# RMS norm on one core: storing the first half tile between the second and the third load, with half tiles alternating from there

## Chip, cores and metric

The kernel runs on one core of one Trainium2 chip. The metric is the device time of one execution in microseconds.

## The reference

The input `x` is 16 x 1024 x 512 in float32, so 16,384 rows of 512 elements and 33.55 MB. Every row is divided by its root mean square and multiplied by `gamma`.

```python
def reference(x, gamma):
    eps = 1e-5
    rms = np.sqrt(np.mean(x ** 2, axis=-1, keepdims=True) + eps)
    return (x / rms * gamma).astype(np.float32)
```

Each byte is read once and written once, 67.1 MB in all, with little arithmetic on it.

## The kernel before

The rows are cut into four tiles of 128 partitions x 32 rows, 8.39 MB each. Three buffers ("slots") hold tiles 0, 1 and 2, and tile 3 goes into slot 0 again. Every load and store is issued by SyncE, in program order. A half tile (16 rows per partition, 4.19 MB) is the unit in which I count below; "store 1a" is the store of the first half of tile 1.

```python
    load(0, 0, 0, 16)          # load(tile, slot, first row, last row)
    load(0, 0, 16, 32)
    load(1, 1, 0, 32)
    load(2, 2, 0, 32)
    ...
    def compute(slot, r0, r1):
        for g in range(r0, r1, G):                 # groups of 8 rows
            ...
            if (g // G) % 2:                       # odd group: two wide squares into PSUM (2 buffers)
                for h in range(0, G, H):
                    sq = psum.tile([P, H, D], fp32, name="sq")
                    nc.scalar.activation(out=sq, in_=slots[slot][:, g + h : g + h + H, :], func=AF.Square)
                    nc.vector.tensor_reduce(out=ss[:, h : h + H], in_=sq, ...)
            else:                                  # even group: eight row squares with their sums, ScalarE alone
                for r in range(G):
                    nc.scalar.activation(out=sq_scratch, ..., func=AF.Square, accum_out=ss[:, r : r + 1])
            nc.scalar.activation(out=rms, in_=ss, func=AF.Sqrt, ...)        # the root, ScalarE
            nc.vector.reciprocal(out=rstd, in_=rms)
            for r in range(G):
                nc.vector.scalar_tensor_tensor(...)                         # one row scaled, in place

    compute(0, 0, 32)
    store(0, 0, 0, 32)
    compute(1, 0, 16)
    store(1, 1, 0, 16)
    load(3, 0, 0, 16)
    load(3, 0, 16, 32)
    compute(1, 16, 32)
    store(1, 1, 16, 32)
    compute(2, 0, 32)
    store(2, 2, 0, 32)
    ...                                            # tile 3 in two halves
```

`sq`, the result of a wide square, has two buffers in PSUM, an on-chip memory: a third wide square waits until VectorE has summed the first.

A scheduler decides in which order each engine gets its instructions. It keeps the data dependences and is otherwise free, so the order on ScalarE and VectorE is not the order of the source.

Of the kernel before, what the change touches and what calls it, by code (L numbers as in the profile page):

```python
# [1 line left out]

# [4 lines left out]


@with_exitstack
def kernel(  # L10
    ctx: ExitStack,
    tc: tile.TileContext,
    x: bass.AP,
    gamma: bass.AP,
    out: bass.AP,
):
    nc = tc.nc
    P = nc.NUM_PARTITIONS
    eps = 1e-5
    fp32 = mybir.dt.float32  # L20
    AF = mybir.ActivationFunctionType
    OP = mybir.AluOpType

    xf = x.flatten_outer_dims()
    of = out.flatten_outer_dims()
    N, D = xf.shape
    R = 32
    G = 8
    H = 4
    assert N == 4 * P * R  # L30

    xv = xf.rearrange("(t p r) d -> t p r d", p=P, r=R)
    ov = of.rearrange("(t p r) d -> t p r d", p=P, r=R)

    const = ctx.enter_context(tc.tile_pool(name="const", bufs=1))
    stats = ctx.enter_context(tc.tile_pool(name="stats", bufs=4))
    psum = ctx.enter_context(tc.tile_pool(name="psum", bufs=2, space=bass.MemoryType.PSUM))

    slots = [const.tile([P, R, D], fp32, name=f"slot{i}") for i in range(3)]

    def load(t, slot, r0, r1):
        nc.sync.dma_start(out=slots[slot][:, r0:r1], in_=xv[t][:, r0:r1])

    def store(t, slot, r0, r1):
        nc.sync.dma_start(out=ov[t][:, r0:r1], in_=slots[slot][:, r0:r1])

    load(0, 0, 0, 16)
    load(0, 0, 16, 32)
    load(1, 1, 0, 32)
    load(2, 2, 0, 32)  # L50

    gamma_row = const.tile([1, D], fp32)
    nc.scalar.dma_start(out=gamma_row, in_=gamma.unsqueeze(0))
    ones_col = const.tile([1, P], fp32)
    nc.vector.memset(ones_col, 1.0)  # L55
    gamma_psum = psum.tile([P, H, D], fp32, name="sq")
    nc.tensor.matmul(gamma_psum[:, 0], ones_col, gamma_row, start=True, stop=True)  # L57
    gamma_b = const.tile([P, D], fp32)
    nc.vector.tensor_copy(out=gamma_b, in_=gamma_psum[:, 0])  # L59

    eps_t = const.tile([P, 1], fp32)
    nc.vector.memset(eps_t, eps)  # L62
    sq_scratch = const.tile([P, D], fp32)

    def compute(slot, r0, r1):
        for g in range(r0, r1, G):
            ss = stats.tile([P, G], fp32, name="ss")
            rms = stats.tile([P, G], fp32, name="rms")
            rstd = stats.tile([P, G], fp32, name="rstd")
            if (g // G) % 2:  # L70
# [3 lines that stand above are left out]
                    nc.vector.tensor_reduce(  # L74
                        out=ss[:, h : h + H], in_=sq, axis=mybir.AxisListType.X, op=OP.add
                    )
            else:
                for r in range(G):
                    nc.scalar.activation(  # L79
                        out=sq_scratch,  # L80
                        in_=slots[slot][:, g + r, :],
                        func=AF.Square,
                        accum_out=ss[:, r : r + 1],
                    )
            nc.scalar.activation(out=rms, in_=ss, func=AF.Sqrt, bias=eps_t, scale=1.0 / D)  # L85
            nc.vector.reciprocal(out=rstd, in_=rms)  # L86
            for r in range(G):
                nc.vector.scalar_tensor_tensor(  # L88
                    out=slots[slot][:, g + r, :],
                    in0=slots[slot][:, g + r, :],  # L90
                    scalar=rstd[:, r : r + 1],
                    in1=gamma_b,
                    op0=OP.mult,
                    op1=OP.mult,
                )

    compute(0, 0, 32)
    store(0, 0, 0, 32)
    compute(1, 0, 16)
    store(1, 1, 0, 16)  # L100
    load(3, 0, 0, 16)
    load(3, 0, 16, 32)
    compute(1, 16, 32)
    store(1, 1, 16, 32)
    compute(2, 0, 32)
    store(2, 2, 0, 32)
    compute(0, 0, 16)
    store(3, 0, 0, 16)
    compute(0, 16, 32)
    store(3, 0, 16, 32)  # L110


# [1 line left out]
_INS = ['x', 'gamma']  # L114
_OUTS = [((16, 1024, 512), 'float32')]


# [23 lines left out]
```

## Time and profile before

| What | Value |
|---|---|
| time | 162.38 us median of 3 (162.14 to 162.44) |
| VectorE busy | 123.4 us, 77% of the span |
| the SyncE queue's share of the 16 DMA engines | 97.9% |
| first half tile landed | 12.80 us |
| last store issued, landed | 147.90 us, about 159.5 us |

These are the head of the page of the kernel before and its DMA queue table (packets, megabytes, share of the span of the 16 engines):

```profile
span 160.6 us, 402 instructions
PE 2.0 (1%) x2; PEld 0.5 (0%) x2; DVE 123.4 (77%) x163; ACT 79.9 (50%) x162; POOL 0.2 (0%) x4
...
q1 hardware_dynamic: 1728, 67.11, 97.9%
q14 instruction: 2, 0.02, 0.0%
```

The next are waits of the kernel before: first VectorE's, then those of SyncE as it issues transfers (who waited for what: total us, times, longest).

```profile
DVE ss L74 <- ACT sq L73: 10.4, 1, 10.4
DVE rstd L86 <- ACT rms L85: 9.8, 4, 5.4
```

```profile
SPq L45 <- DVE slot L88: 113.7, 6, 28.3
...
SPq L136 <- DMA out_dram<-slot: 11.3, 2, 9.6
```

Two things end nearly together. The queue is busy from start to end. And the last store, which waits for VectorE's last multiply, is issued at 147.90 us; with 0.33 us to issue it and 11.3 us of waiting at the end, it lands at 159.5 us. VectorE is idle mainly for two reasons (and after its last multiply): it waits 10.4 us for the first data, and in all 9.8 us for ScalarE's root (line 86), one of these waits being 5.4 us.

This is VectorE's timeline in the kernel before where it goes from tile 1 to tile 2 (start, duration, operation; an idle time would stand in brackets at the end of the line):

```profile
82.67 0.26 DVE L86 RECIPROCAL rstd<-rms 128x8 f32<-128x8 f32 x2
82.89 10.69 DVE L88 SCALAR_TENSOR_TENSOR slot<-slot,rstd,gamma_b 128x512 f32<-128x512 f32 x16
93.50 4.48 DVE L74 TENSOR_REDUCE ss<-sq 128x4 f32<-128x2048 f32 x2
97.89 0.26 DVE L86 RECIPROCAL rstd<-rms 128x8 f32<-128x8 f32 x2
```

There is no bracket: VectorE does not wait here.

```profile
117.04 0.34 SPq L45 DMA_DIRECT2D out_dram<-slot  x1
...
147.90 0.33 SPq L45 DMA_DIRECT2D out_dram<-slot  x1
```

### The profile page before, as it was taken

The numbers are of one execution on the slowest core, as the hardware profiler recorded it, in microseconds if no ns is written. First come the engines' busy times: TensorE is split into PE (matmuls) and PEld (weight loads), VectorE is DVE, ScalarE is ACT, GpSimd is POOL, SyncE is SP. The second block draws the span as 40 slices with busy tenths as digits, with TensorE's granted clock in tenths as the row PEclk, the third lists the DMA queues.
The fourth block names the chain that finished last, engine by engine and source line by source line (L and its number), as shares of the span: only waits on it lengthen the run. The fifth ranks groups of instructions, "written<-read, shape, count | busy, mean of one in ns | idle before, by whom it ended". The sixth has DMA issues, their size and how long they took to land.

```text
span 160.6 us, 402 instructions
## 1 busy us (share of the span) xinstructions
PE 2.0 (1%) x2; PEld 0.5 (0%) x2; DVE 123.4 (77%) x163; ACT 79.9 (50%) x162; POOL 0.2 (0%) x4
## 2 busy tenths in 40 slices
PE   4000000000000000000000000000000000000000
PEld 1000000000000000000000000000000000000000
DVE  0101909999999509999999999998999999998000
ACT  3008999930580999995099314003998960000000
POOL 0000000000000000000000000000000000000000
DMA  7999999969969997997999999999997997999993
GB/s 262 392 408 498 400 408 506 522 261 522 522 263 522 506 278 345 441 522 310 473 392 416 465 416 416 473 416 408 457 547 310 506 490 310 416 465 408 433 457 155
DMA packets 1732, 67.13 MB, mean 418 GB/s; under 512 B 193, under 2 KB 193, under 8 KB 194
## 3 DMA queue, kind: packets, MB, share of 16 engines
q1 hardware_dynamic: 1728, 67.11, 97.9%
q14 instruction: 2, 0.02, 0.0%
q10 hardware_dynamic: 2, 0.00, 0.0%
HBM read 33.56 MB, written 33.55 MB: 418 GB/s over the span
## 4 chain that ended last, share of the span: by engine, by line
DVE 71%; ACT 12%; DMA 8%; issue 1%; DVEq 0%
DVE slot L88 52%; DVE ss L74 18%; DMA slot<-in_x_dram 8%; ACT sq_scratch L79 6%; ACT sq L73 4%; DVE rstd L86 1%; ACT L85 1%; ACT rms L85 1%; DVEq L136 0%
## 5 line engine op out<-in xcount | busy, mean ns | idle before, releaser
L88 DVE SCALAR_TENSOR_TENSOR slot<-slot,rstd,gamma_b 128x512 f32<-128x512 f32 x128 | 85.7, 746 | 0.1
L79 ACT ACTIVATE sq_scratch<-slot 128x512 f32<-128x512 f32 x64 | 40.0, 625 | 13.9 <-DMA slot<-in_x_dram 12.6
L74 DVE TENSOR_REDUCE ss<-sq 128x4 f32<-128x2048 f32 x16 | 36.1, 2276 | 10.5 <-ACT sq L73 10.4
L73 ACT ACTIVATE sq<-slot 128x2048 f32<-128x2048 f32 x16 | 29.8, 1860 | 4.9 <-DVE ss L74 4.9
L85 ACT ACTIVATE rms<-ss,eps_t 128x8 f32<-128x8 f32 x16 | 4.4, 297 | 37.4 <-DVE ss L74 37.2
L79 ACT ACTIVATION_READ_ACCUMULATOR sq_scratch<-slot 128x1 f32 x64 | 11.9, 187 | 0.0
L86 DVE RECIPROCAL rstd<-rms 128x8 f32<-128x8 f32 x16 | 2.8, 188 | 9.8 <-ACT rms L85 9.8
L59 DVE COPY gamma_b<-sq 128x512 f32<-128x512 f32 x1 | 0.7, 692 | 3.2 <-PE sq L57 3.2
L57 PE MATMUL sq<-gamma_row,ones_col 1*128 1x512 f32 x2 | 2.0, 1122 | 2.2 <-DMA gamma_row<-in_gamma_dram 2.2
L79 ACT ACT_TABLE_LOAD x1 | 1.3, 1283 | 1.3 <-PEq L125 1.3
L85 ACT ACT_TABLE_LOAD x1 | 1.3, 1283 | 0.0
L55 DVE MEMSET ones_col<- 1x128 f32 x1 | 0.2, 165 | 0.8 <-PEq L125 0.8
L57 PEld LDWEIGHTS sq<-gamma_row,ones_col 1*128 1x128 f32 x2 | 0.5, 305 | 2.1 <-issue 2.1
L125 POOL MEMSET const-bfloat16-1.0<- 128x1 bf16 x1 | 0.1, 102 | 0.0
L125 POOL MEMSET const-uint8-127<- 128x1 uint8 x1 | 0.1, 102 | 0.0
L125 POOL MEMSET const-float32-0.0<- 128x1 f32 x1 | 0.1, 99 | 0.2 <-issue 0.2
L125 POOL MEMSET const-float32-1.0<- 128x1 f32 x1 | 0.1, 99 | 0.0
L62 DVE MEMSET eps_t<- 128x1 f32 x1 | 0.1, 59 | 0.0
## 6 DMA issues: line engine op xcount, KB each, us to landing
slot<-in_x_dram SPq DMA_DIRECT2D x4, 4096.0 KB, 19.3
out_dram<-slot SPq DMA_DIRECT2D x4, 4096.0 KB, 18.0
slot<-in_x_dram SPq DMA_DIRECT2D x2, 50.5
out_dram<-slot SPq DMA_DIRECT2D x2, 27.6
gamma_row<-in_gamma_dram ACTq DMA_DIRECT2D x1, 2.0 KB
```

The source lines that it names most:

```text
L55: nc.vector.memset(ones_col, 1.0)
L57: nc.tensor.matmul(gamma_psum[:, 0], ones_col, gamma_row, start=True, stop=True)
L59: nc.vector.tensor_copy(out=gamma_b, in_=gamma_psum[:, 0])
L62: nc.vector.memset(eps_t, eps)
L73: nc.scalar.activation(out=sq, in_=slots[slot][:, g + h : g + h + H, :], func=AF.Square)
L74: nc.vector.tensor_reduce(out=ss[:, h : h + H], in_=sq, axis=mybir.AxisListType.X, op=OP.add)
L79: nc.scalar.activation(out=sq_scratch, in_=slots[slot][:, g + r, :], func=AF.Square, accum_out=ss[:, r : r + 1],)
L85: nc.scalar.activation(out=rms, in_=ss, func=AF.Sqrt, bias=eps_t, scale=1.0 / D)
L86: nc.vector.reciprocal(out=rstd, in_=rms)
L88: nc.vector.scalar_tensor_tensor(out=slots[slot][:, g + r, :], in0=slots[slot][:, g + r, :], scalar=rstd[:, r : r + 1], in1=gamma_b, op0=O ...
L125: nc = _bacc.Bacc("TRN2", target_bir_lowering=False, num_devices=1)
```

## The change

The intent is to begin storing early: the first half of tile 0 is stored before tile 2 is loaded, and from there loads and stores of half tiles alternate in the queue.

```diff
     load(0, 0, 0, 16)
     load(0, 0, 16, 32)
     load(1, 1, 0, 32)
-    load(2, 2, 0, 32)
 ...
-    compute(0, 0, 32)
-    store(0, 0, 0, 32)
+    compute(0, 0, 16)
+    store(0, 0, 0, 16)
+    load(2, 2, 0, 32)
+    compute(0, 16, 32)
+    store(0, 0, 16, 32)
+    load(3, 0, 0, 16)
     compute(1, 0, 16)
     store(1, 1, 0, 16)
-    load(3, 0, 0, 16)
     load(3, 0, 16, 32)
     compute(1, 16, 32)
     store(1, 1, 16, 32)
```

No arithmetic changes. The queue's order goes from `L0a L0b L1 L2 | S0 S1a L3a L3b S1b S2 S3a S3b` to `L0a L0b L1 | S0a L2 S0b L3a S1a L3b S1b S2 S3a S3b`.

The order of instructions on ScalarE and VectorE changes as well, and the diff does not show that. With `r` for a row square, `w` for a wide square, `s` for a root (ScalarE), `t` for the sum of a wide square, `q` for a reciprocal and `m` for a row scaled (VectorE), and the number of the group of 8 rows behind the letter (groups 4 to 7 are tile 1, 8 to 11 tile 2), the built programs read, from the end of tile 1 into tile 2:

```
ScalarE before:  r6x8 s6 r8 w9 r8x7 r10 s7 s8 w9 r10 w11 r10x6 s9 s10 w11 s11
ScalarE after:   r6x8 s6 s7 r8 w9 r8 w9 r8 w11 r8 w11 r8x4 s8 s9 r10x8 s10
VectorE before:  m5x8 m6x8 t7 t9 q7 q8 m7x8 m8x8 t9 t11 q9 q10 m9x8 ...
VectorE after:   m5x8 m6x8 t7 q7 m7x8 t9x2 q8 t11 m8x8 q9 q10 m9x8 ...
```

## The prediction

> **What bounds the kernel now.** Two things that finish almost together. (1) The DMA queue. Every transfer sits on SyncE's one queue: by the queue table 97.9% of the 16 engines' span, 418 GB/s. By the waits the first half tile (4.19 MB) lands at 12.80 us, and the last store, issued at 147.9, takes 11.6 us (shortest issue to landing), so it lands near 159.5: fifteen half tiles in 146.7 us, 9.78 us each, with no hole. (2) VectorE, 123.4 us busy. Its last multiply ends at 147.88 and releases the last store just as the queue runs out (SyncE's last waits, 11.3 us, fit the store before it landing near 149.9). So there is almost no slack for a VectorE delay.
>
> **What the change does.** Same bytes, same instructions on ScalarE and VectorE; one more DMA issue. The third load goes behind the first half store, so it lands near 72 instead of 62 us; the first load of tile 3 lands near 92 instead of 102. SyncE's stream stays supplied: I find store 0a issued at 34.7 (queue full until 41), store 0b at 50, load 3a at 52, store 1a at 73, load 3b at 82. The Trainium skill, "DMA: Bandwidth & Descriptors", "Queues, rings and completion order", has descriptors consumed in ring order on each engine; the landings of before (12.8, 22.5, 41.9, about 62) agree. By itself the reorder gains and loses nothing; loads and stores both take about 9.8 us.
>
> **What I expect to cost time.** The comparison of instruction orders shows that the scheduler also re-orders ScalarE and VectorE for tile 2. In before, ScalarE gives tile 2 one wide square, then all eight row squares and the root, so VectorE passes from tile 1 to tile 2 without a pause. In after, tile 2 repeats the pattern of tile 1: four wide squares come before the last four row squares, and there are two PSUM buffers, so the third wide square waits for a VectorE reduction queued behind tile 1's last multiplies. VectorE does two reductions, and its next instruction is the reciprocal that needs ScalarE's root: it waits for wide, row, wide, four rows, root (1.8, 0.65, 1.8, 4 x 0.755, 0.3 us). The same pattern is in the trace before 59.85 us: VectorE idle 5.40 us. I expect a second such hole, 5.4 us, at about 91 to 96 us.
>
> Replaying both orders with the trace's durations (an estimate) reproduces before (VectorE end 148.0, measured 147.9) and gives for after: tile 1 finished at 86.5 (88.3 before), hole 90.8 to 96.3, tile 2 finished at 124.9 (117.0 before), VectorE end 153.8. The queue, empty after store 1b at about 120, idles about 6 us until store 2; then four half tiles follow: 124.9 + 0.9 + 4 x 9.8 + about 1 = 166 landing, against 159.5. All of the hole is on the critical path.
>
> **Prediction:** 162.4 + 5.8 = 168.2 us; 8 in 10 within 166.6 to 169.4. Faster by over 2%: 0.01; within 2%: 0.07; slower by over 2%: 0.92.
>
> **Right if:** the waits show VectorE's reciprocal waiting about 5.4 us for ScalarE's root twice (total near 15 instead of 9.8); VectorE busy unchanged at 123.4 us; store 2 issued near 125; DMA slices drop near 120 to 126 us; span near 166.5; queue share near 94%.
>
> **Wrong if:** alternating shortens the 9.8 us per half tile; the hole is shorter because ScalarE gets ahead while waiting; load 3a waits for both halves of slot 0; or the later tile 2 starves ScalarE (it needs it only by about 80 us).

## More of the kernel before

All runs told here are in the undisturbed state: granted clock 1.0 (full speed), and the repeats of one kernel mostly within half a per cent of each other. The experiments ran on several chips (1, 4 and 7), so each is compared with runs of the kernel before in its own rounds.

Last, two stretches of 4 us (the last two columns are the DMA share and GB/s; a packet is booked where it ends, so single stretches scatter around 1) and the issue of store 2 and of the last store, of the kernel before:

```profile
120.00:124.00 4.00, 0.00 (x0) 0.00 (x0) 3.74 (x7) 3.42 (x7) 0.00 (x0) 1.00 0.95 410
124.00:128.00 4.00, 0.00 (x0) 0.00 (x0) 4.00 (x7) 3.94 (x9) 0.00 (x0) 1.00 1.21 524
```

## The result, and the profile after

The changed kernel takes 167.73 us (median of 4, 167.65 to 167.80) and the kernel before 162.41 us in the same rounds. The ratio is 1.033, with a 95% interval of 1.0312 to 1.0348: slower. Ratios in this document are the mean time of one kernel's fast runs over that of the other's in the same rounds, so they are not quite the ratio of the medians quoted.

The head of the page and the queue table of the changed kernel:

```profile
span 166.0 us, 404 instructions
PE 2.0 (1%) x2; PEld 0.5 (0%) x2; DVE 123.6 (74%) x163; ACT 79.9 (48%) x162; POOL 0.2 (0%) x4
...
q1 hardware_dynamic: 1872, 67.11, 94.9%
q14 instruction: 2, 0.02, 0.0%
```

Its waits, first VectorE's and then SyncE's:

```profile
DVE rstd L85 <- ACT rms L84: 15.5, 6, 5.4
DVE ss L73 <- ACT sq L72: 10.5, 1, 10.5
```

```profile
SPq L45 <- DVE slot L87: 125.1, 7, 37.8
...
SPq L138 <- DMA out_dram<-slot: 10.7, 2, 9.6
```

VectorE works as long as before (123.6 against 123.4 us), but it waits 15.5 instead of 9.8 us for roots. Its timeline in the changed kernel, from tile 1 to tile 2, shows where:

```profile
81.23 5.39 DVE L87 SCALAR_TENSOR_TENSOR slot<-slot,rstd,gamma_b 128x512 f32<-128x512 f32 x8
86.54 4.48 DVE L73 TENSOR_REDUCE ss<-sq 128x4 f32<-128x2048 f32 x2
96.41 0.20 DVE L85 RECIPROCAL rstd<-rms 128x8 f32<-128x8 f32 x1 [5.39 <-ACT rms L84]
```

The bracket says that VectorE stood idle for 5.39 us before the reciprocal, until the root on line 84 was done. What ScalarE did meanwhile is in its own timeline of the changed kernel:

```profile
86.21 0.18 ACT L78 ACTIVATION_READ_ACCUMULATOR sq_scratch<-slot 128x1 f32 x1
88.85 1.88 ACT L72 ACTIVATE sq<-slot 128x2048 f32<-128x2048 f32 x1 [2.46 <-DVE ss L73]
90.67 0.61 ACT L78 ACTIVATE sq_scratch<-slot 128x512 f32<-128x512 f32 x1
...
91.28 1.86 ACT L72 ACTIVATE sq<-slot 128x2048 f32<-128x2048 f32 x1
...
96.08 0.49 ACT L84 ACTIVATE rms<-ss,eps_t 128x8 f32<-128x8 f32 x2
```

The third wide square of tile 2 found both PSUM buffers full. It waited 2.46 us, until VectorE, done with tile 1, had summed the first. Only then could ScalarE do that wide square, a row, another wide square, four rows and the root. VectorE had nothing else in its order but the reciprocal that needs that root.

The consequence for the queue, in the two stretches and the two issues of the changed kernel that answer to those of before:

```profile
120.00:124.00 4.00, 0.00 (x0) 0.00 (x0) 4.00 (x7) 0.00 (x0) 0.00 (x0) 1.00 0.04 16
124.00:128.00 4.00, 0.00 (x0) 0.00 (x0) 4.00 (x7) 0.00 (x0) 0.00 (x0) 1.00 0.61 262
```

```profile
124.87 0.34 SPq L45 DMA_DIRECT2D out_dram<-slot  x1
...
153.90 0.33 SPq L45 DMA_DIRECT2D out_dram<-slot  x1
```

Store 2 is issued 7.8 us later than before (124.87 against 117.04). The queue has run dry and moves 16 GB/s from 120 to 124 us. The last store is issued 6.0 us later (153.90 against 147.90), and the span is 5.4 us longer.

### The profile page after: what moved, and what is told of

The parts are those of the page before. It is cut to its first block, busy times and chain, and to the rows that moved or that the text cites. A ratio compares the mean times of both kernels' runs of the same rounds, so it can differ in the third digit from the quotient of the medians.

```text
span 166.0 us, 404 instructions
## 1 busy us (share of the span) xinstructions
PE 2.0 (1%) x2; PEld 0.5 (0%) x2; DVE 123.6 (74%) x163; ACT 79.9 (48%) x162; POOL 0.2 (0%) x4
## 4 chain that ended last, share of the span: by engine, by line
DVE 67%; ACT 16%; DMA 7%; issue 1%; DVEq 0%
DVE slot L87 50%; DVE ss L73 16%; ACT sq_scratch L78 8%; DMA slot<-in_x_dram 7%; ACT sq L72 7%; ACT rms L84 1%; DVE rstd L85 1%; ACT L84 1%; DVEq L138 0%
## 5 line engine op out<-in xcount | busy, mean ns | idle before, releaser
L85 DVE RECIPROCAL rstd<-rms 128x8 f32<-128x8 f32 x16 | 2.8, 191 | 15.5 <-ACT rms L84 15.5
```

## The experiments

My theory was that the time is lost by the order of the compute instructions in tile 2, and that the order of the transfers is neutral in itself. The rival was that the transfers cost it: tile 2 lands ten microseconds later, and the queue alternates. The first two runs each change one of the two orders and keep the other. Each time is beside runs of the kernel before in the same rounds.

### e1 and e2: the two orders swapped

Both kernels are written with the orders of the two engines as lists. Every ScalarE and VectorE instruction is pinned behind the one before it in the list by an order-only edge (no waiting is added). The instructions and their operands are the same. In their traces both engines run the same sequence of operations as in before (e1) and in the changed kernel (e2).

```diff
-    compute(0, 0, 16)
-    store(0, 0, 0, 16)
-    ...
+    ACT_ORDER = expand("r0 w1 r0 w1 r0x6 s0 s1 ... r6x8 s6 r8 w9 r8x7 r10 s7 s8 w9 ...")   # e1: order of before
+    DVE_ORDER = expand("t1x2 q0 q1 m0x8 m1x8 ... m6x8 t7 t9 q7 q8 m7x8 m8x8 ...")
+    DMA_ORDER = [("load", 0, 0, 16), ("load", 0, 16, 32), ("load", 1, 0, 32),
+                 ("store", 0, 0, 16), ("load", 2, 0, 32), ("store", 0, 16, 32), ...]       # e1: order of after
+    ...
+        i = nc.scalar.activation(...)
+        tc.keep_in_program_order(i)
```

In e2 it is the other way round: the lists of the changed kernel, the transfers of before.

> The new transfer order, with every ScalarE and VectorE instruction pinned in the order of the kernel before. Theory (the loss is the re-ordered compute of tile 2): no VectorE hole near 91 us, VectorE waits for ScalarE's root 9.8 us in all, store 2 issued near 117, time 162.4 us (161.9 to 162.9). Rival (the transfer order itself, tile 2 ten us later and alternating directions, costs the 5.3 us): near 167.7 us. A share for each would land between.

> The transfer order of the kernel before, with ScalarE and VectorE pinned in the order of the changed kernel. Theory: the hole of 5.4 us stands although tile 2 lands at 62 us again, store 2 issued near 125, time 167.7 us (167.0 to 168.6). Rival (late data of tile 2): near 162.4 us.

| Kernel | transfers | compute order | time us | ratio to before (95%) |
|---|---|---|---|---|
| changed kernel (its own rounds) | new | new | 167.73 | 1.0330 (1.0312 to 1.0348) |
| e2 | old | new | 167.69 | 1.0328 (1.0304 to 1.0352) |
| e1 | new | old | 164.72 | 1.0135 (1.0119 to 1.0151) |
| before (rounds of e1 and e2) | old | old | 162.55 | 1 |

e2 is the theory's number exactly: with the old transfers, the new compute order alone costs everything that the change costs. The wait of VectorE is the same, first as its total and then in the timeline of e2:

```profile
DVE rstd L120 <- ACT rms L104: 15.5, 6, 5.4
```

```profile
96.23 0.20 DVE L120 RECIPROCAL rstd<-rms 128x8 f32<-128x8 f32 x1 [5.39 <-ACT rms L104]
```

e1 contradicts half of the theory. With the old compute order, the new transfers should have been free, 161.9 to 162.9 us, and they cost 2.2 us. The waits of e1 show that compute is not to blame:

```profile
ACT sq_scratch L97 <- DMA slot<-in_x_dram: 20.7, 3, 10.3
...
DVE rstd L120 <- ACT rms L104: 9.8, 4, 5.4
```

ScalarE waits 20.7 us for data where the kernel before waits 12.6, so the late tile 2 is felt there. But VectorE waits as before, and the issues of store 2 and of the last store in e1 are where they were (117.04 and 147.90 before):

```profile
117.09 0.34 SPq L45 DMA_DIRECT2D out_dram<-slot  x1
...
147.92 0.33 SPq L45 DMA_DIRECT2D out_dram<-slot  x1
```

The final wait of SyncE is what grew, from 11.3 to 13.5 us:

```profile
SPq L186 <- DMA out_dram<-slot: 13.5, 2, 9.6
```

So two costs exist, and they do not add up: 2.2 and 5.1 us alone, 5.3 together. The first had to be explained.

### e3 and e4: the transfers alone

All compute is left out, so the results are wrong; the order of the queue stays.

```diff
-    compute(0, 0, 16)
     store(0, 0, 0, 16)
     load(2, 2, 0, 32)
-    compute(0, 16, 32)
     store(0, 0, 16, 32)
     ...
```

> Only the loads and stores of the changed kernel, no compute (the result is wrong on purpose). Theory: transfers do not care for the order: sixteen half tiles at 9.8 us plus about 3 us of start and end, 162 us, within 0.5 us of the copy in the old order. Rival (alternating has its own price or bonus): a difference of over 1 us between the two copies.

> Only the loads and stores of the kernel before, no compute (the result is wrong on purpose). Theory: 162 us, the same as the whole kernel before (162.4), which would show that kernel to be at the floor of its own transfers. If VectorE were what bounds the kernel before, this would be clearly shorter, by over 2 us.

e3 took 162.63 us (ratio 1.0002, 0.9974 to 1.0031) and e4 162.16 us (0.9978, 0.9962 to 0.9995). Two things follow. The kernel before is within 0.3% of its own bare transfers: no reordering of its compute could have gained more. And the bare new order costs at most about 0.5 us (the two intervals overlap), not the 2.2 of e1. Alternating in itself is not the whole reason.

### What the landings say

A transfer of this size is split over 16 DMA engines, and each adds one to the transfer's semaphore when its share has landed; the Trainium skill ("DMA: Bandwidth & Descriptors", "Why a DMA increments its semaphore by 16 and not by 1") says that only the full 16 means that all has landed. The trace records these 16 landings. I call the latest of the 16 minus their median the lag. At the last store:

| Kernel | turns from load to store | lag us | span us | span minus lag us |
|---|---|---|---|---|
| before | 2 | 0.46 | 160.6 | 160.1 |
| e4, bare, old transfers | 2 | 0.39 | 160.2 | 159.8 |
| e3, bare, new transfers | 4 | 0.75 | 160.8 | 160.0 |
| e1, new transfers, old compute order | 4 | 2.76 | 162.9 | 160.1 |

Without the lag all four would take the same within 0.3 us. In e1 fifteen engines are within 0.31 us of the median and one is 2.76 us late. The lag after each transfer in e1, in order of landing, grows from load to load (1.19, 1.96 and 2.84 us at loads 2, 3a and 3b), with smaller values at the stores between:

```
e1:      0.35 0.35 0.26 0.26 1.19 0.74 1.96 1.67 2.84 2.79 2.77 2.78 2.76
before:  0.23 0.21 0.22 0.56 0.55 0.20 0.57 0.58 0.53 0.54 0.54 0.46
```

In e1's packet records (a 32 KB packet takes 1.21 us, a 64 KB packet 2.42 us), an 8 KB instruction fetch begins at 64.2 us and one data packet at that time takes 0.55 us longer (another fetch, at 47.2 us, cost a packet only 0.11). Then one packet takes 0.54 us longer near 69.9 us, one 0.76 us near 89.8 and one 0.86 us near 109.9, and no other packet there more than 0.21: just where the queue turns from loading to storing for the second, third and fourth time. The one near 69.9 us is a 64 KB packet, which at that place only tile 2's load has. So the late engine seems to lose in its last packet of a load, when the others already store. In the first turn all 16 engines lose about the same (1.05 to 1.6 us in one packet each), so it makes no lag. The records name no engine; that these packets are all of the late engine is inferred from the steps of the lag. The sums fit: 0.11 + 0.55 + 0.54 = 1.20 us, with 0.76 more 1.96 and with 0.86 more 2.82, against lags of 1.19, 1.96 and 2.84 at the three loads.

The bare copies fetch no instructions during the run: their queue tables have no line for the instruction queue, while those of before and after have one with 2 packets. That suggested the next pair.

### e11 and e12: the bare transfers with unrelated work beside them

The copies of e3 and e4, with as many ScalarE and VectorE instructions as the real kernel, on tiles that no transfer touches.

```diff
+    side = const.tile([P, H, D], fp32)
+    nc.vector.memset(side, 1.0)
+    for g in range(16):
+        ...                 # squares, sums, root, reciprocal, eight scalings, reading side alone
     store(0, 0, 0, 16)
     load(2, 2, 0, 32)
     store(0, 0, 16, 32)
     ...
```

> The copy in the new transfer order with as many instructions on ScalarE and VectorE as the real kernel, but on tiles of their own, so that no transfer waits for them (wrong result on purpose). It asks where the 2.2 us come from that the new transfer order cost with the old compute order but not in the bare copy. Theory: one of the 16 engines is held up by two 8 KB instruction fetches (the bare copy has none) and loses more at each turn from loading to storing; then the last engine's landing trails the middle one by about 2 to 3 us as in the real kernel (0.7 in the bare copy) and the time is near 164.5 us. Rival (it is the late issue of the stores, a queue with little behind it): lag near 0.7, time near 162.6.

> The same with the old transfer order, as a control. Theory: two turns from loading to storing instead of four, so little lag, 0.5 to 1.2 us, time 162.3 to 163. If the side work costs by itself (contention for SBUF), both copies would be slower by the same amount.

e11 took 164.51 us (1.0115, 1.0092 to 1.0138) with a lag of 2.68 us; e12 took 162.64 us (1.0009, 0.9983 to 1.0034) with a lag of 0.28 us. Span minus lag is 160.1 and 160.0 us. So the rival, that stores issued late make the queue slow, falls: in e11 the first three are issued within 0.1 us of those of e3, and the fourth 1.5 us later (84.12 against 82.59), far from the late stores of e1. Neither side work alone (e12) nor the new transfers alone (e3) cost much; together they cost 2 us. The queue table of e11 has the instruction fetches again:

```profile
q1 hardware_dynamic: 1872, 67.11, 96.7%
q14 instruction: 2, 0.02, 0.0%
```

That the fetches, rather than some other effect of running instructions, set the one engine back is supported by the time of the first long packet in e1 (and in e11, where a fetch at 57.2 us goes with a packet that is 0.60 us too long). The kernel before shows it too: fetches at 45.9 and 64.1 us, with one packet 0.33 and one 0.36 us too long. It is not proved by a run that removes the fetches alone; in e12, for one, the second fetch (58.3 us) falls into the first turn, where all engines lose time. Why an engine that is behind loses again at a turn stays open, and it does not at every turn: the second turn of the kernel before leaves the lag as it was (0.57 us at load 3a, 0.58 at load 3b, 0.53 at store 1b), and the fourth of e11 adds 0.09 us (2.59 at load 3a, 2.68 at load 3b).

### e9 and e10: which part of the change does what

e9 is the kernel before with only tile 2's load moved behind the first half store. e10 is the changed kernel with only that load moved back.

```diff
 # e9, from before                        # e10, from after
-    load(2, 2, 0, 32)                    +    load(2, 2, 0, 32)
     ...                                       ...
+    compute(0, 0, 16)                         compute(0, 0, 16)
+    store(0, 0, 0, 16)                        store(0, 0, 0, 16)
+    load(2, 2, 0, 32)                    -    load(2, 2, 0, 32)
```

> The kernel before with tile 2's load behind the first half store, and the store of tile 0 therefore in halves, but tile 3's two loads left together behind store 1a as before. The scheduler gives tile 2 the order of the changed kernel. Theory: hole of 5.4 us, store 2 issued near 123 (before the first piece of tile 3, unlike the changed kernel), last store near 154: 167.5 us (166.8 to 168.2). Rival (the alternation of the later half tiles costs): near 162.4.

> The changed kernel with tile 2's load back among the first loads; half stores and alternating loads of tile 3 kept. The scheduler gives tile 2 the order of before. Theory: no second hole, last store near 147.7, 162.5 us (162.0 to 163.2). Rival (alternation of half tiles costs): near 167.7.

e9 took 167.72 us (1.0312, 1.0290 to 1.0334), the whole loss. e10 took 163.60 us (1.0055, 1.0033 to 1.0076); it was expected at 163.2 at most. In e10 the last store is issued at 147.43 us, and the lag is 1.79 us with three turns: span minus lag is again 160.1. So it is the place of tile 2's load in the program that makes the scheduler reorder the start of tile 2 (the built orders of e9 and e10 show that too). The lag cannot be put down to one of the two parts: e9, without the alternating loads of tile 3, also has three turns, and its lag reaches 2.16 us at store 1b before the empty queue hides it (0.09 us at store 2).

### e5: mending the order in the changed kernel

In tile 2, the second wide square of a group goes behind the root of the group before it; the rest of the source is the changed kernel's.

```diff
+                    if slot == 2 and h == H:
+                        tc.add_manual_dep(wide.ins, last_root[-1].ins.name, <order only>, ...)
                     nc.vector.tensor_reduce(
```

> The changed kernel with two ordering edges of one kind: in tile 2, the second wide square of a group goes behind the root of the row-squared group before it. Theory: the hole at 91 us goes (VectorE waits for roots about 10 us in all instead of 15.5), store 2 issued near 120, time 163.1 us (162.4 to 163.7), a little over before because store 2 starts near the moment the queue runs out. Rival (transfer order): stays near 167.7.

e5 took 164.24 us (1.0090, 1.0051 to 1.0129). The hole is gone; the waits for roots are back at the 9.8 us of before (the last figures of this line):

```profile
L95 DVE RECIPROCAL rstd<-rms 128x8 f32<-128x8 f32 x16 | 2.9, 192 | 9.8 <-ACT rms L93 9.8
```

Store 2 is issued at 119.53 us and the last store at 148.17 us. Two edges take the ratio from 1.033 to 1.009. The time misses the expected 163.7 at most: the expectation did not know the lag, 1.62 us here. Span minus lag is 160.6, half a microsecond above the others: store 2 came a little late, as expected, and only 7 data packets were in flight at 120.2 us, where the kernel before keeps 16.

### e6: store 2 in halves

```diff
-    compute(2, 0, 32)
-    store(2, 2, 0, 32)
+    compute(2, 0, 16)
+    store(2, 2, 0, 16)
+    compute(2, 16, 32)
+    store(2, 2, 16, 32)
```

> The changed kernel with the store of tile 2 in two halves. The hole stays, but the first half of tile 2 is stored from about 109.5 us, so the queue should not run dry at 120. Theory: the last store is still issued at 153.9 and needs 11.6 us, so the time falls only by what the queue was behind at the end, 0.3 to 1 us: 167.0 us (166.5 to 167.6). If the empty queue at 120 to 125 were the cause in itself, it would fall to near 162.4.

e6 took 167.55 us (1.0293, 1.0250 to 1.0335), as expected. The same two stretches as above, and a later one, in e6:

```profile
120.00:124.00 4.00, 0.00 (x0) 0.00 (x0) 4.00 (x8) 0.00 (x0) 0.00 (x0) 1.00 1.04 451
124.00:128.00 4.00, 0.00 (x0) 0.00 (x0) 4.00 (x8) 0.00 (x0) 0.00 (x0) 1.00 0.95 410
148.00:152.00 4.00, 0.00 (x0) 0.00 (x0) 4.00 (x7) 0.00 (x0) 0.00 (x0) 1.00 0.15 66
```

The queue no longer runs dry at 120 us; it runs dry in the stretch from 148 us instead (empty from 151.2 to 154.6 us), waiting for the last store, which VectorE releases at 153.79 us. The empty queue at 120 us was a symptom. VectorE's late end is the cause.

### e7 and e8: can the kernel before be beaten?

e7 has the old transfers and an order in which tile 1 too loses its hole at 54 to 60 us, written as lists like e1. e8 is e7 with the loads of tiles 0 to 2 issued by ScalarE.

```diff
 # e7, ScalarE's and VectorE's lists against those of before
-    r4 w5 r4 w5 r4 w7 r4 w7 r4x4 s4 s5 r6x8 s6       t5x2 q4 t7 m4x8 q5 q6
+    r4 w5 r4x7 s4 w5 r6 w7 r6x7 s5 s6 w7             t5 q4 m4x8 t5 t7 q5 q6
 # e8, from e7
-        return nc.sync.dma_start(out=slots[slot][:, r0:r1], in_=xv[t][:, r0:r1])
+        return (nc.scalar if t < 3 else nc.sync).dma_start(out=slots[slot][:, r0:r1], in_=xv[t][:, r0:r1])
```

> The transfer order of before, with compute of tile 1 pinned so that its hole of 5.4 us at 54 to 60 goes too. VectorE ends near 142.7 instead of 147.9. Theory (before is bounded by its transfers): no gain, 162.3 us (161.9 to 162.7), the slack of VectorE before its last store grows to 5 us. If VectorE bounded the kernel before, it would gain 5 us: 157.

> As the run without holes, with the first loads issued from ScalarE's queue and the stores and last loads from SyncE's, so that a store no longer stands behind the loads. If the limit is the 16 engines or the memory, not the single queue: the same, 162.3 us (161.5 to 163). If one queue limits the rate: faster by over 2%.

e7 took 163.47 us (1.0038, 1.0000 to 1.0076). Its last store is issued at 142.56 us, 5.3 us earlier than before, and nothing is gained; it even misses the expected 162.7 with a lag of 1.16 us. e8 took 162.97 us (1.0012, 0.9977 to 1.0047): two issuing queues are no faster than one. The Trainium skill ("DMA: Bandwidth & Descriptors", "Issuing engines are not separate DMA queues") says that transfers run on the same 16 engines whichever engine started them, and this agrees. No run that does the work beat the kernel before, and e4 says why: its bare transfers take 0.9978 of that time.

## Why the prediction was right, and where it was not

- **The hole.** Predicted: a second wait of 5.4 us, at about 91 to 96 us. Measured: 5.39 us, ending at 96.41; waits for roots 15.5 us (predicted near 15), VectorE busy 123.6 us (unchanged, as predicted). e2 shows that the order of compute alone makes it, and e5 that mending the order removes it.
- **The critical path.** Predicted: all of the hole counts. Measured: the last store is issued 6.0 us later, the time is 5.3 us longer. The prediction reckoned the end by the queue, as store 2 and four half tiles behind it. e6 lets the first half of store 2 go 15 us earlier and takes 167.55 us against 167.73, so VectorE's end bounds the time as tightly.
- **The tail.** Predicted: store 2 issued near 125 and the last landing at 166. Measured: 124.87, and 165.07 (the latest of the 16 landings in the trace). I costed the last four half tiles at 9.8 us each, the mean of the whole run, plus 0.9 and about 1; from the issue of store 2 to the last landing they took 40.2 us instead of 41.1. The landing was thus reckoned 6.5 us later than before and came 5.5 us later; for the time I put 5.8 us, and 5.3 us were measured.
- **"By itself the reorder gains and loses nothing."** This step failed. e1 shows that the new transfers cost 2.2 us (1.35%) when the compute order is kept. The prediction took the 9.78 us per half tile as a property of the transfers. It did not see that a transfer ends with the slowest of 16 engines, and that one of them falls behind by 2.8 us in the new order. In the changed kernel this cost is hidden. Its lag is 2.64 us when store 1b lands, and 0.10 us at store 2, because the queue stands empty meanwhile and the late engine catches up. So the predicted time was right although one cost was missed: on this point it was right by luck.
- **"It needs it only by about 80 us."** Right: tile 2's late landing made ScalarE wait in e1, but moved no store.

## What to carry to other kernels

Moving a load in the source can reorder compute engines that do not depend on it; compare the built instruction orders before and after, not the diff alone. In a kernel that is bound by its transfers, look at the latest of the 16 landings and not the mean rate: in e1 each of the last three loads, just before a turn to storing, left one engine further behind, up to 2.84 us, and in the changed kernel the lag was gone (0.10 us) after the queue had stood empty. Two costs that each show alone need not add: the larger one can hide the smaller by making the slack in which it is absorbed, so swap the halves of a change both ways before calling either half free.

## What the Trainium skill lacked or had wrong

- "DMA: Bandwidth & Descriptors" has nothing on turning a queue from loads to stores. Here the first turn lengthened one packet on each of the 16 engines by 1.05 to 1.6 us (e1), and each of the three later turns one packet by 0.54 to 0.86 us (e1); in e11 no packet at the fourth turn was as much as 0.2 us longer.
- The same page, "Latency and other measured facts", explains the slow single DMA engines 7 and 15, as a best guess, by transfers issued from GpSimd. Here all transfers came from SyncE, and one engine of 16 still ended up to 2.76 us after the median (e1); which engine it was the trace does not say.
- "Runtime: NRT & Kernel Launch", "Instruction fetch mechanics", calls the cost of fetching "mostly hidden" and speaks of 16 KiB blocks. Here two 8 KB fetch packets of 0.31 us fall in the middle of a run; one data packet at a fetch took 0.55 us longer (e1), and the kernels with fetches and four turns reached lags of 2.0 to 2.8 us (e6, e5, changed kernel, e11, e1) where the bare copy e3 had 0.75. That the fetch is the reason is supported, not proved.
- The bandwidth table of "DMA: Bandwidth & Descriptors" has 425 GB/s for a 16 MB load and no row for loads and stores together. Here the bare copy e4, half loads and half stores, moved 419 GB/s over its span, nearly the same.
